# Five low halves written ahead in the output projection, six low halves of the query phase on GpSimd, a fifth head searched early, in a one-core transformer block

## The chip, the cores and the metric

One core of a Trainium2 chip runs the whole block in one launch. The metric is the device time of the program in microseconds, the median over several executions; lower is better. Engines: PE (TensorE, matmuls), DVE (VectorE), ACT (ScalarE), POOL (GpSimd), SP (SyncE, which only issues transfers here).

## The reference

512 tokens of width 1024, in float32. After a mixer, 128 x 128 experts of one neuron each are retrieved for every token by product keys: 8 heads, the 16 best of 128 in each of two halves, the 16 best of their 256 sums.

```python
def reference(x, c, ...):
    ada = silu(c) @ w_ada + b_ada          # shift, scale, gate of both sub-layers
    h = modulate(rmsnorm(x, norm1_g), sh1, sc1)
    z = h @ w_in                            # 2560 columns
    y_a = gate_b * causal_dwconv(gate_c * xa, conv_a_w)
    xr = causal_dwconv(xr, conv_b_w) + conv_b_b
    y_b = rg_lru(xr, ...) * gelu(gr)
    y = concat(head_rmsnorm(y_a), head_rmsnorm(y_b)) @ w_out
    x = x + g1 * y
    h = modulate(rmsnorm(x, norm2_g), sh2, sc2)
    x = x + g2 * peer(h, w_q, sub_keys, expert_u, expert_v)
    return rmsnorm(x, final_g)

def block(xb):                              # of peer, 128 tokens
    q = (xb @ w_q).reshape(p, 8, 2, 64)
    sc = einsum('phcd,hcnd->phcn', q, sub_keys)
    top_s, top_i = top_k(sc, 16)
    ...                                     # the 16 best of 256 sums: idx, g = softmax
    act = gelu(einsum('phkd,pd->phk', expert_u[idx], xb))
    return einsum('phk,phkd->pd', g * act, expert_v[idx])
```

## The kernel before, in words

**Split products.** A float32 product is made from halves: `high` (ACT, line 74) rounds a weight block of 128 x 1024 to fp32r as `whi`, `low` (DVE, line 79) takes `wraw - whi` as `wlo`, and `mm3` multiplies high by high (L88), high by the activations' low (L89) and low by high (L90), for each of 8 pieces of the inner width: 24 matmuls a chunk. `split_w` is high and low in a row. Rings of four buffers hold `wraw`, `whi` and `wlo`.

**Stages in order.**

1. adaLN, norm, the input projection in 20 chunks (`zblock`), the mixer and its head norms, which write `ybuf_h` and `ybuf_l` (L504) in four parts. The parts of adaLN that are needed later (`ada_rest`: rows of `norm2`, and `ada_gate2` for the second gate) go as a generator between other work: pieces of `w_ada` are loaded, multiplied and summed on DVE (L163), summed over partitions by PE (L138), copied by ACT, transposed by PE (L146) and added to `adac` by DVE (L150).
2. The output projection: eight chunks m of `w_out`, 24 matmuls of 512 columns each into `ps_z`. DVE then adds the gated product to the residual, `xs[m]` (L618, for the last chunk L628), ACT squares it, DVE sums the squares (`sqa`, L221). `qsp[0]`, the halves of the first query head, are made behind the loop. Until chunk 6 the program's scheduler places the instructions; the last chunk and the norm behind it stand under a manual schedule, where an engine's order is the order written.
3. The second norm: sums of the squares over partitions (L204), `rs_m` and the reciprocal root (L635 to L640), eight times four transposes of `xs` (L588) for `x1d`, a copy of the residual in DRAM, and the modulated `h2h`, `h2l`, `h2f` (full precision).
4. The query phase: eight heads, each with a chunk of `w_q`, `qT` (ACT, L728), its scores against the keys (L732) and, on DVE, searches of the 16 best (`top16`, L690 to L699: twice MAX8, FIND_INDEX8 and MATCH_REPLACE8 for each half). `qsp[h + 1]` is split during head h. The searches of the first HQ = 4 heads, four tiles of 128 tokens each, are done here (`early`), the others in the next stage.
5. The U phase: 128 chunks of `expert_u` (chunk 0 in the query phase) for the 320 tokens that are computed densely, into `ps_act`, then gelu on ACT. Chunks 1 to FN - 1 = 11 are not split: full float32 matmuls from `h2f` (L1159), which need no work of DVE or ACT on the weights; the others are split. Beside them DVE does the remaining searches, the gates, and dots (L1066) with rows of `expert_u` that POOL gathers (L1045) for the tokens that are computed sparsely. A planner sets the order of this DVE work ahead of time: it adds estimated costs (`pe[0]` by FPE or 3530 ns for a chunk, `dve[0]` by 1140 for a low) and, after each chunk, `turn` picks work as long as DVE's estimated time is behind PE's.
6. The V phase: 128 chunks of `expert_v` into `acc` (L1336 to L1345), for 384 tokens. DVE makes `wlo`, and for two chunks at a time the coefficients `cf` (L1222) and their low half `cl` (L1236); between them stand the remaining dots (L1066) and the weighted sums of gathered rows (L1083), spread evenly. Then the end.

The loads that matter go by SP's queue; gathers and `x1d` by POOL's.

## Time and profile before

| what | us |
|---|---|
| median of 3 runs (1328.17 to 1332.12) | 1329.12 |
| the profiled execution | 1328.57 |
| its span, first to last instruction | 1326.8 |
| mean granted clock of PE, share of full speed | 0.996 |

A row of the page's or a view's timeline reads: start, length, engine, line, operation, output<-inputs, shape, and in brackets the idle time before it and what ended it. Matmuls overlap, so the distance between starts counts and not the length: 0.23 us for 512 columns at the end of the output projection, 0.147 us for the split U chunks. "x8" at a row's end joins eight equal instructions. In the table of stretches every engine has its busy time and, in brackets, its instructions. The page's slices show the stages: PE at 9 from the second slice to the last but one, DMA at 8 or 9 from the eleventh on.

```profile
PE   8999999999999999999999999999999999999995
...
DVE  6889976999999999999999689899899989899998
...
DMA  9765542163898999999999999999999999999993
```

### The profile page before, as it was taken

To read this page: it belongs to the slowest core of one execution; us is meant where nothing else is said; L and a number is where in the kernel's file an instruction comes from. 1 tells how busy PE (TensorE), PEld (TensorE's weight loads), DVE (VectorE), ACT (ScalarE), POOL (GpSimd) and SP (SyncE) were. 2 spreads that over 40 slices of the span, in tenths; PEclk is the share of its full clock that TensorE was granted. 3 is DMA by queue.
4 is the path that set the end of the run, shared out by engine and by line. 5 is a ranking of instruction groups with operands and counts; after the bars stand their busy time and mean duration, and the time that the engine had idled before them with its cause. 6 is when DMAs were issued, how large, how long until landed. Compare 5 with 4: busy or idle time off the path is not lost.

```text
span 1326.8 us, 21286 instructions
## 1 busy us (share of the span) xinstructions
PE 1304.6 (98%) x7506; PEld 1127.3 (85%) x7506; DVE 1215.5 (92%) x2247; ACT 728.2 (55%) x1319; POOL 503.8 (38%) x336
## 2 busy tenths in 40 slices
PE   8999999999999999999999999999999999999995
PEld 6677777777999999999999998788888888888884
DVE  6889976999999999999999689899899989899998
ACT  4677636424586898878669543334343434343432
POOL 0000001000244121446655356677554656554560
PEclk9999999999999999999999999999999999999998
DMA  9765542163898999999999999999999999999993
GB/s 369 272 242 174 185 133 101 59 210 102 302 355 297 341 326 348 394 366 416 417 413 399 402 358 410 377 408 418 412 415 413 415 412 416 412 415 411 416 401 134
DMA packets 150267, 440.05 MB, mean 332 GB/s; under 512 B 16016, under 2 KB 43664, under 8 KB 150160
## 3 DMA queue, kind: packets, MB, share of 16 engines
q1 hardware_dynamic: 103008, 267.23, 53.9%
q0 software_dynamic: 46864, 170.41, 32.5%
q8 instruction: 59, 0.97, 0.3%
q10 hardware_dynamic: 288, 1.05, 0.2%
q14 instruction: 48, 0.39, 0.1%
HBM read 393.54 MB, written 45.09 MB: 331 GB/s over the span
## 4 chain that ended last, share of the span: by engine, by line
PE 56%; DMA 13%; issue 13%; DVE 12%; POOL 3%; ACT 2%; SPq 1%; DVEq 0%; POOLq 0%; ACTq 0%
DMA wraw<-in_v_dram 10%; PE ps_act L88 10%; PE ps_act L89 9%; PE ps_act L90 9%; PE ps_z L89 4%; PE ps_z L90 4%; PE ps_z L88 4%; PE ps_act L1159 4%; PE ps_gt L908 3%; POOL rows L1045 3%; DVE ys L1083 2%; DVE scr L1066 2%; DVE cl L1236 2%; PE acc L1345 2%; DVE wlo L79 2%
## 5 line engine op out<-in xcount | busy, mean ns | idle before, releaser
L74 ACT ACTIVATE whi<-wraw 128x1024 fp32r<-128x1024 f32 x255 | 269.7, 1058 | 217.6 <-DMA wraw<-in_v_dram 148.3
L79 DVE TENSOR_TENSOR wlo<-wraw,whi 128x1024 fp32r<-128x1024 f32 x255 | 310.5, 1218 | 41.9 <-ACT whi L74 41.4
L88 PE MATMUL ps_act<-h,whi 128*128 128x320 f32 x928 | 291.5, 314 | 0.0
L89 PE MATMUL ps_act<-h,whi 128*128 128x320 f32 x928 | 286.8, 309 | 0.0
L90 PE MATMUL ps_act<-h,wlo 128*128 128x320 f32 x928 | 286.7, 309 | 0.0
L1045 POOL DMA_INDIRECT rows<-in_u_dram,idx_s x128 | 204.8, 1600 | 131.1 <-DVE scr L1066 105.4
L1045 POOL DMA_INDIRECT rows<-in_v_dram,idx_s x128 | 197.0, 1539 | 143.8 <-DVE ys L1083 122.4
L1345 PE MATMUL acc<-whi,cl 128*128 128x512 f32 x744 | 230.0, 390 | 1.6 <-DVE cl L1236 1.4
L1345 PE MATMUL acc<-whi,ch 128*128 128x512 f32 x744 | 229.2, 389 | 0.0
L1345 PE MATMUL acc<-wlo,ch 128*128 128x512 f32 x744 | 229.1, 389 | 0.0
L1045 POOL DMA_INDIRECT rows<-in_u_dram,idx_b x64 | 95.7, 1495 | 237.9 <-DVE scr L1066 179.3
L89 PEld LDWEIGHTS ps_act<-h,whi 128*128 128x128 f32 x928 | 174.4, 188 | 0.2
L88 PEld LDWEIGHTS ps_act<-h,whi 128*128 128x128 f32 x928 | 174.2, 188 | 0.3
L90 PEld LDWEIGHTS ps_act<-h,wlo 128*128 128x128 f32 x928 | 174.2, 188 | 0.0
L1345 PEld LDWEIGHTS acc<-whi,cl 128*128 128x128 f32 x744 | 139.1, 188 | 33.0 <-DVE cl L1236 4.5
L1083 DVE SCALAR_TENSOR_TENSOR ys<-rows,acts,ys 128x1024 f32<-128x1024 f32 x127 | 163.3, 1286 | 1.6
L1345 PEld LDWEIGHTS acc<-wlo,ch 128*128 128x128 f32 x744 | 139.7, 188 | 29.1
L1345 PEld LDWEIGHTS acc<-whi,ch 128*128 128x128 f32 x744 | 139.5, 188 | 28.8
L1066 DVE SCALAR_TENSOR_TENSOR scr<-rows,h2n 128x1024 f16<-128x1024 f32 x128 | 156.2, 1220 | 5.3 <-DMA rows<-in_u_dram,idx_s 3.6
L1150 ACT ACTIVATE act<-ps_act 128x320 f32<-128x320 f32 x127 | 55.9, 440 | 125.6 <-PE ps_act L90 92.8
L896 ACT ACTIVATE igh<-oh,gl 128x128 f16<-128x128 f16 x320 | 99.7, 440 | 0.0
L595 POOL DMA_DIRECT2D x1d<-xn x8 | 4.6, 581 | 214.7 <-ACT xn L594 214.7
(325 smaller groups left out, 1921.6 us busy)
## 6 DMA issues: line engine op xcount, KB each, us to landing
wraw<-in_uT_dram SPq DMA_DIRECT2D x120, 512.0 KB, 7.2
wraw<-in_v_dram SPq DMA_DIRECT2D x103, 512.0 KB, 13.4
Gd<-stg SPq DMA_DIRECT2D x46, 512.0 KB, 8.4
wada<-in_w_ada_dram SPq DMA_DIRECT2D x45, 512.0 KB, 6.1
Ad<-act SPq DMA_DIRECT2D x48, 320.0 KB, 6.6
act<-Ad SPq DMA_DIRECT2D x48, 320.0 KB, 15.0
raw<-in_v_dram SPq DMA_DIRECT2D x25, 512.0 KB, 13.4
h<-Gd SPq DMA_DIRECT2D x12, 1024.0 KB, 18.3
```

What stands on the lines that cost most here:

```text
L74: nc.scalar.activation(hi, raw, AF.Copy)
L79: nc.vector.tensor_sub(lo, raw, hi.bitcast(F32))
L88: nc.tensor.matmul(ps, hi[:, k, :], xh(k), start=first and k == ks[0], stop=False)
L89: nc.tensor.matmul(ps, hi[:, k, :], xl(k), start=False, stop=False)
L90: nc.tensor.matmul(ps, lo[:, k, :], xh(k), start=False, stop=last and k == ks[-1])
L896: nc.scalar.activation(ig[:, 1, k // 2, :, k % 2], of[:, k // 2, 0, :, k % 2], AF.Copy, scale=gl[:, t0 + k:t0 + k + 1])
L1045: nc.gpsimd.indirect_dma_start(out=r[:, :], out_offset=None, in_=table, in_offset=bass.IndirectOffsetOnAxis(ap=idxs[:, k:k + 1], axis=0))
L1066: nc.vector.scalar_tensor_tensor(scr, rows.pop(n), 1.0, hn, op0=OP.mult, op1=OP.mult, accum_out=dst[:, k:k + 1])
L1083: nc.vector.scalar_tensor_tensor(ys, rows.pop(k), acts[:, k:k + 1], ys, op0=OP.mult, op1=OP.add)
L1150: nc.scalar.activation(act[c // 2][:, c % 2], ps, AF.Gelu)
L1159: nc.tensor.matmul(ps, raw[:, j, :], h2f[j // 2][:, j % 2], start=j == 0, stop=j == KB - 1)
L1345: nc.tensor.matmul(accs[b][e], st[:, bs], mv[:, e * 512:(e + 1) * 512], start=first, stop=last)
```

## The change

It has five parts.

- `low` and `split_w` can name an engine. In the query phase the low halves of heads 3 to 7 and of U chunk 0 (six) go to GpSimd.
- The output projection is written out under the manual schedule from chunk 1 on. Its first two chunks are split before the loop, `ada_rest` is drained before it, `xs` and the sums of a chunk follow one chunk later, and the second gate is a generator with its pieces loaded two ahead, whose steps stand between the chunks (L195 for L163).
- In it, U chunks 1 to PM = 5 are loaded, split, and their low halves stored in DRAM (`Ld`, 512 KB each) by POOL's queue; `low_ahead` does it.
- In the U phase chunks 1 to 5 are split: the raw block is loaded and rounded by ACT as before for others, the low half is loaded from `Ld` by SP. FN goes from 12 to 14, so full-float32 chunks are now 6 to 13, eight for eleven. The planner's costs follow.
- HQ goes from 4 to 5, with seven search steps in a head for six.

```diff
--- before.py
+++ after.py
@@ -74,14 +74,14 @@
         nc.scalar.activation(hi, raw, AF.Copy)
         return hi
 
-    def low(raw, hi):
+    def low(raw, hi, eng=None):
         lo = wring.tile([128, KB, 128], FR, name="wlo", bufs=WB)
-        nc.vector.tensor_sub(lo, raw, hi.bitcast(F32))
+        (eng or nc.vector).tensor_sub(lo, raw, hi.bitcast(F32))
         return lo
 
-    def split_w(raw):
+    def split_w(raw, eng=None):
         hi = high(raw)
-        return hi, low(raw, hi)
+        return hi, low(raw, hi, eng)
 
     def mm3(ps, hi, lo, xh, xl, ks, first, last):
         for k in ks:
@@ -186,10 +186,20 @@
         yield
 
     def ada_gate2():
-        acc = yield from ada_sum(3, 1)
+        acc = first.pop(3)
+        wts = [None] + [piece(k, 3) for k in (1, 2)]
+        yield
+        nc.vector.tensor_scalar(acc, acc, cl[:, 0:1], None, op0=OP.mult)
+        for k in range(1, KB):
+            yield
+            nc.vector.scalar_tensor_tensor(acc, wts[k], cl[:, k:k + 1], acc, op0=OP.mult, op1=OP.add)
+            if k + 2 < KB:
+                wts.append(piece(k + 2, 3))
         pr = ada_rows()
+        yield
         for b in range(2):
             row_mm(pr, b, ones, acc, True, True)
+        yield
         ada_cols(pr, 40, 8)
         nc.sync.dma_start(g2d.rearrange("b (m p) -> p (b m)", p=128), adac[:, 40:48])
         yield
@@ -458,7 +468,6 @@
                 next(gate1, None)
             next(norm2, None)
             yield
-        yield from ada_gate2()
     ada_it = ada_rest()
 
 
@@ -594,30 +603,53 @@
         nc.scalar.activation(xn, pt, AF.Copy)
         nc.gpsimd.dma_start(x1d[t * 128:(t + 1) * 128, e * 512:(e + 1) * 512], xn)
 
-    osp = {}
-    qraw, qsp = {}, {}
+    osp = {m: split_w(oraw[m]) for m in range(2)}
+    qraw, qsp, uraw = {}, {}, {}
+    Ld = dram.tile([PM, 128, D], F32, name="Ld")
+    for _ in ada_it:
+        pass
+    first[3] = piece(0, 3, "wacc", 2)
+    gate2 = ada_gate2()
+    next(gate2)
+
+    def low_ahead(c):
+        raw = uraw.pop(c)
+        lo = low(raw, high(raw))
+        nc.gpsimd.dma_start(Ld[c - 1], lo.bitcast(F32).rearrange("p k e -> p (k e)"))
+
+    psm = {}
+    norm2 = ExitStack()
     for m in range(KB):
+        if m == 1:
+            norm2.enter_context(tc.manual_schedule())
         if m + 2 < KB:
             oraw[m + 2] = load_w(w_out[m + 2])
         else:
             qraw[m + 2 - KB] = load_w(w_q[m + 2 - KB])
-        if m < KB - 1:
-            osp[m] = split_w(oraw[m])
-        if m >= KB - 2:
-            for _ in ada_it:
-                pass
-            osp[KB - 1] = osp.get(KB - 1) or split_w(oraw[KB - 1])
+        if 1 <= m <= PM:
+            uraw[m] = load_w(uT[m])
         if m == KB - 1:
-            norm2 = ExitStack()
-            norm2.enter_context(tc.manual_schedule())
+            next(gate2)
         hi, lo = osp.pop(m)
-        ps = psZ.tile([128, T], F32, name="ps_z", bufs=3)
-        mm3(ps, hi, lo, lambda k: ybuf_h[:, k, :], lambda k: ybuf_l[:, k, :], kord, True, True)
+        psm[m] = psZ.tile([128, T], F32, name="ps_z", bufs=3)
+        mm3(psm[m], hi, lo, lambda k: ybuf_h[:, k, :], lambda k: ybuf_l[:, k, :], kord, True, True)
+        if m == 0:
+            continue
+        p = m - 1
+        nc.vector.scalar_tensor_tensor(xs[:, p, :], psm.pop(p), adac[:, 16 + p:17 + p], xs[:, p, :], op0=OP.mult,
+                                       op1=OP.add)
+        if 2 <= m + 1 < KB:
+            osp[m + 1] = split_w(oraw[m + 1])
         if m == KB - 1:
-            break
-        nc.vector.scalar_tensor_tensor(xs[:, m, :], ps, adac[:, 16 + m:17 + m], xs[:, m, :], op0=OP.mult, op1=OP.add)
-        sq_sum(m, True)
-        next(ada_it, None)
+            next(gate2)
+        sq_sum(p, True)
+        for _ in range({1: 2, 6: 2}.get(m, 1 if m < 6 else 0)):
+            next(gate2)
+        if m - 1 in uraw:
+            low_ahead(m - 1)
+    if KB - 1 in uraw:
+        low_ahead(KB - 1)
+    ps = psm.pop(KB - 1)
     mx.close()
     adx.close()
     qp = pro.enter_context(tc.tile_pool(name="qp", bufs=2))
@@ -717,7 +749,7 @@
         else:
             qraw[h + 2] = load_w(uT[h - 6])
         if h:
-            qsp[h + 1] = split_w(qraw[h + 1])
+            qsp[h + 1] = split_w(qraw[h + 1], nc.gpsimd if h > 1 else None)
         hi, lo = qsp[h]
         ps = psZ.tile([128, T], F32, name="ps_z", bufs=3)
         mm3(ps, hi, lo, lambda k: h2h[:, k, :], lambda k: h2l[:, k, :], range(KB), True, True)
@@ -731,7 +763,7 @@
             for c in range(2):
                 nc.tensor.matmul(pss[c][:, t, :], qT[64 * c:64 * c + 64, t * 128:(t + 1) * 128],
                                  keys_sb[64 * c:64 * c + 64, h, :], start=True, stop=True)
-        for _ in range(6 if h >= 2 else 0):
+        for _ in range(7 if h >= 2 else 0):
             next(early, None)
         for c in range(2):
             sc[h, c] = scs.tile([128, NT, 128], F32, name="sc", bufs=SCB)
@@ -1100,7 +1132,7 @@
     def w_load(k):
         if k < len(jobs):
             kind, i = jobs[k]
-            if 5 <= k < FN:
+            if 4 + PM < k < FN:
                 raw = wring.tile([128, KB, 128], FR, name=("wlo", "whi")[k % 2], bufs=WB).bitcast(F32)
                 nc.sync.dma_start(raw, uT[i])
                 wraw[k] = raw
@@ -1114,11 +1146,18 @@
                              v[vorder[i] * 128:(vorder[i] + 1) * 128, :].rearrange("p (k e) -> p k e", k=KB))
 
     def w_high(k):
-        if FN <= k < len(jobs):
+        if k <= PM or FN <= k < len(jobs):
             whi[k] = high(wraw[k])
 
+    def low_load(k):
+        if k <= PM:
+            wlo[k] = wring.tile([128, KB, 128], FR, name="wlo", bufs=WB)
+            nc.sync.dma_start(wlo[k].bitcast(F32).rearrange("p k e -> p (k e)"), Ld[k - 1])
+
     def w_low(k):
-        if FN <= k < len(jobs):
+        if k <= PM:
+            wraw.pop(k)
+        elif FN <= k < len(jobs):
             wlo[k] = low(wraw.pop(k), whi[k])
             settle()
 
@@ -1131,6 +1170,7 @@
 
     def weights(k):
         w_ahead(k)
+        low_load(k + 3)
         w_low(k + 2)
 
     act = {0: act0}
@@ -1153,7 +1193,7 @@
         c = jobs[k][1]
         if c:
             ps = pool.tile([128, NU], F32, name="ps_act", bufs=3 if pool is psE else 2)
-            if k < FN:
+            if PM < k < FN:
                 raw = wraw.pop(k)
                 for j in range(KB):
                     nc.tensor.matmul(ps, raw[:, j, :], h2f[j // 2][:, j % 2], start=j == 0, stop=j == KB - 1)
@@ -1164,9 +1204,9 @@
         q = c // 2 - 2
         if c % 2 == 0 and 0 <= q < v0 // 2:
             spill(q)
-        pe[0] += FPE if c and k < FN else 3530
-        dve[0] += 0 if c and k < FN - 2 else 1140
-        ac[0] += 450 if c and k < FN - 3 else 1400
+        pe[0] += FPE if PM < k < FN else 3530
+        dve[0] += 0 if k < FN - 2 else 1140
+        ac[0] += 450 if PM - 3 < k < FN - 3 else 1400
 
     gbuf, g16, gdone = {}, {}, set()
     coef = {}
@@ -1268,6 +1308,7 @@
         w_load(k)
     for k in range(1, 3):
         w_high(k)
+        low_load(k)
     w_low(1)
     manual = ExitStack()
     manual.enter_context(tc.manual_schedule())
@@ -1443,7 +1484,8 @@
 GS = 32768.0
 AB = 3
 GPE = 460
-FN = 12
+FN = 14
+PM = 5
 DX = 0.3
 FPE = 4400
 SE = 0.65
@@ -1468,7 +1510,7 @@
 WB = 4
 WR = 4
 SCB = 8
-HQ = 4
+HQ = 5
 VT = 4
 NW = 32
 
```

What this does to the order of instructions is shown at three places. On DVE as a whole, 278 low halves stand for 281, 51 dots stand ahead of the first `cl` for 47, and 205 of the sparse steps (dots and sums) stand behind it for 209; POOL gets five stores and six subtractions, SP five loads.

**First place, DVE at the start of the output projection.** Before, from the last step of the head norms (L504); the names are those of the stages above.

```order
L163 SCALAR_TENSOR_TENSOR wacc<-wada,cl_104,wacc 128x1024
L504 TENSOR_TENSOR ybuf_l<-mfull,ybuf_h 128x512
L134 MEMSET ps_row 128x512
L618 SCALAR_TENSOR_TENSOR xs<-ps_z,adac,xs 128x512 x3
L79 TENSOR_TENSOR wlo<-wraw,whi 128x1024
L221 TENSOR_TENSOR sqa<-sqa,sq 128x512
L79 TENSOR_TENSOR wlo<-wraw,whi 128x1024
```

And in the changed kernel, where L513 is that step, L639 the `xs` step, L231 the sum of squares and L192 and L195 the second gate:

```order
L513 TENSOR_TENSOR ybuf_l<-mfull,ybuf_h 128x512
L639 SCALAR_TENSOR_TENSOR xs<-ps_z,adac,xs 128x512
L79 TENSOR_TENSOR wlo<-wraw,whi 128x1024
L192 TENSOR_SCALAR wacc<-wacc,cl_104 128x1024
L195 SCALAR_TENSOR_TENSOR wacc<-wada,cl_104,wacc 128x1024
L639 SCALAR_TENSOR_TENSOR xs<-ps_z,adac,xs 128x512
L79 TENSOR_TENSOR wlo<-wraw,whi 128x1024
```

Three `xs` steps stood together behind three chunks that PE worked on in turn; now the first stands alone, and the low half of chunk 2 behind it. The steps of adaLN that stood between those of the head norms (L163) have moved.

**Second place, the end of the output projection.** DVE before, to the second norm's `rs_m`:

```order
L618 SCALAR_TENSOR_TENSOR xs<-ps_z,adac,xs 128x512
L221 TENSOR_TENSOR sqa<-sqa,sq 128x512
L628 SCALAR_TENSOR_TENSOR xs<-ps_z,adac,xs 128x512
L630 TENSOR_TENSOR sq<-xs 128x512
L635 TENSOR_SCALAR rs_m<-ps_col 128x4
```

DVE in the changed kernel, where L660 is the last chunk's `xs` step, L662 its square and L667 `rs_m`; the second low half shown is that of the first query head:

```order
L195 SCALAR_TENSOR_TENSOR wacc<-wada,cl_104,wacc 128x1024 x2
L134 MEMSET ps_row 128x512
L79 TENSOR_TENSOR wlo<-wraw,whi 128x1024
L639 SCALAR_TENSOR_TENSOR xs<-ps_z,adac,xs 128x512
L150 TENSOR_TENSOR adac<-ps_row,small_sb 128x8
L231 TENSOR_TENSOR sqa<-sqa,sq 128x512
L79 TENSOR_TENSOR wlo<-wraw,whi 128x1024
L660 SCALAR_TENSOR_TENSOR xs<-ps_z,adac,xs 128x512
L662 TENSOR_TENSOR sq<-xs 128x512
L667 TENSOR_SCALAR rs_m<-ps_col 128x4
```

PE at the same place before, from the last product:

```order
L90 MATMUL ps_z<-ybuf_h,wlo 128x512
L204 MATMUL ps_col<-ones,sqa 128x1 x4
L588 MATMUL ps_z<-ident,xs 128x128 x8
L204 MATMUL ps_col<-ones,sq 128x1 x4
L588 MATMUL ps_g<-ident,xs 128x128 x8
```

And PE in the changed kernel (L214 for L204, L597 for L588):

```order
L90 MATMUL ps_z<-ybuf_h,wlo 128x512
L146 MATMUL ps_row<-ident,wada 128x128 x4
L214 MATMUL ps_col<-ones,sqa 128x1 x4
L597 MATMUL ps_z<-ident,xs 128x128 x8
L214 MATMUL ps_col<-ones,sq 128x1 x4
L597 MATMUL ps_g<-ident,xs 128x128 x8
```

The second gate's four transposes have moved from the middle of a chunk to behind the last one, and DVE's add that takes them, a sum of squares and a low half stand ahead of the last `xs` step.

**Third place, DVE late in the V phase.** Before, between the 57th and the 58th `cl`:

```order
L1236 TENSOR_TENSOR cl<-cf,ch 128x768
L79 TENSOR_TENSOR wlo<-wraw,whi 128x1024
L1222 TENSOR_TENSOR cf<-act,h_9622 128x2x320
L1083 SCALAR_TENSOR_TENSOR ys<-rows,acts,ys 128x1024 x2
L79 TENSOR_TENSOR wlo<-wraw,whi 128x1024
L1083 SCALAR_TENSOR_TENSOR ys<-rows,acts,ys 128x1024 x2
L1236 TENSOR_TENSOR cl<-cf,ch 128x768
```

And in the changed kernel between the same two (L1276 for L1236, L1262 for L1222, L1115 for L1083):

```order
L1276 TENSOR_TENSOR cl<-cf,ch 128x768
L79 TENSOR_TENSOR wlo<-wraw,whi 128x1024
L1262 TENSOR_TENSOR cf<-act,h_9734 128x2x320
L1115 SCALAR_TENSOR_TENSOR ys<-rows,acts,ys 128x1024
L79 TENSOR_TENSOR wlo<-wraw,whi 128x1024
L1115 SCALAR_TENSOR_TENSOR ys<-rows,acts,ys 128x1024 x2
L1276 TENSOR_TENSOR cl<-cf,ch 128x768
```

One of four sums is gone from this pair of chunks; the rows behind it are as before, up to the end.

## The prediction

> **What bounds the kernel now.** I read the page's busy times first, then the table by stretches, then the list of waits and the rows of single stretches.
>
> ```profile
> PE 1304.6 (98%) x7506; PEld 1127.3 (85%) x7506; DVE 1215.5 (92%) x2247; ACT 728.2 (55%) x1319; POOL 503.8 (38%) x336
> ...
> 200.00:225.00 25.00, 24.09 (x145) 18.25 (x143) 15.62 (x29) 15.15 (x26) 4.63 (x8) 1.00 0.28 106
> 225.00:250.00 25.00, 24.58 (x147) 18.96 (x149) 21.54 (x106) 14.25 (x22) 0.00 (x0) 1.00 0.27 85
> 250.00:275.00 25.00, 25.00 (x149) 20.11 (x148) 25.00 (x152) 7.09 (x13) 0.00 (x0) 1.00 0.24 85
> 275.00:326.00 51.00, 51.00 (x213) 37.07 (x212) 49.20 (x302) 17.07 (x23) 1.12 (x2) 1.00 0.47 153
> 326.00:600.00 274.00, 274.00 (x2156) 270.51 (x2155) 268.97 (x606) 217.75 (x479) 86.76 (x59) 1.00 0.93 338
> 600.00:900.00 300.00, 298.98 (x1918) 276.24 (x1917) 269.84 (x368) 173.83 (x373) 179.53 (x113) 1.00 1.02 400
> 900.00:1200.00 300.00, 299.40 (x1318) 246.64 (x1317) 281.64 (x289) 117.65 (x149) 177.28 (x114) 1.00 1.03 414
> 1200.00:1300.00 100.00, 97.13 (x428) 80.18 (x427) 95.67 (x89) 39.54 (x50) 53.90 (x36) 1.00 1.01 401
> ```
>
> PE is the bound: the columns after the stretch's length are PE, PE's weight loads, DVE, ACT, POOL, granted clock, DMA share, GB/s. From 326 to 1300 PE is idle only 1.0 + 0.6 + 2.9 = 4.5 us, and all of it comes after 600. DVE is the near second: full at 250–275, and 97% in the first split chunks (268.97 of 274). So the change can gain in two ways only: by less PE work, or by removing those 4.5 us. It can lose wherever DVE is made late enough for PE to wait.
>
> **Term 1, three fewer full-precision chunks.** PE work of the U phase:
>
> ```profile
> 279.44 0.81 PE L1159 MATMUL ps_act<-act,wraw 128*128 128x320 f32 x2
> ...
> 326.67 0.55 PE L88 MATMUL ps_act<-h,whi 128*128 128x320 f32 x1
> 327.06 0.31 PE L89 MATMUL ps_act<-h,whi 128*128 128x320 f32 x1
> ...
> 330.57 0.31 PE L89 MATMUL ps_act<-h,whi 128*128 128x320 f32 x1
> ```
>
> The eleven unsplit chunks (1 to 11) take 326.67 − 279.44 = 47.23 us, 4.29 each. A split chunk is 24 matmuls: from the second of one to the second of the next is 330.57 − 327.06 = 3.51. Afterwards eight chunks are unsplit (6 to 13) and three more are split: 3 × (4.29 − 3.51) = **−2.3 us**. Matmuls run back to back here, so the bounds are narrow (−2.2 to −2.4) as long as the low halves are there.
>
> Chunks 1 to 5 get theirs from DRAM: five stores on POOL's queue and five loads on SP's, 512 KB each.
>
> ```profile
> x1d<-xn POOLq DMA_DIRECT2D x8, 256.0 KB, 2.4
> wraw<-in_uT_dram SPq DMA_DIRECT2D x12, 512.0 KB, 3.8
> ```
>
> These are the landing times between 150 and 330 us. Twice the first row is 4.8 us for a store, the second gives 3.8 for a load. Stores come before 207, loads after 270, and the DMA share there is 0.28 to 0.47, so I cost them at nothing. If a load were late, PE would wait for it at one chunk, some 4 us at most.
>
> **Term 2, the output projection and its tail.** What DVE and PE do at its end now:
>
> ```profile
> 197.51 0.17 DVE L150 TENSOR_TENSOR adac<-ps_row,small_sb 128x8 f32<-128x8 f32 x1 [1.75 <-PE ps_row L146]
> ...
> 202.08 0.75 DVE L618 SCALAR_TENSOR_TENSOR xs<-ps_z,adac,xs 128x512 f32<-128x512 f32 x1 [3.81 <-PE ps_z L90]
> 203.59 0.69 DVE L221 TENSOR_TENSOR sqa<-sqa,sq 128x512 f32<-128x512 f32 x1 [0.76 <-ACT sq L219]
> 207.52 0.75 DVE L628 SCALAR_TENSOR_TENSOR xs<-ps_z,adac,xs 128x512 f32<-128x512 f32 x1 [3.24 <-PE ps_z L90]
> 208.30 0.69 DVE L630 TENSOR_TENSOR sq<-xs 128x512 f32<-128x512 f32 x1
> 210.14 0.16 DVE L635 TENSOR_SCALAR rs_m<-ps_col 128x4 f32<-128x4 f32 x1 [1.15 <-PE ps_col L204]
> ```
>
> ```profile
> 196.87 0.60 PE L146 MATMUL ps_row<-ident,wada 128*128 128x128 f32 x4
> ...
> 207.09 0.39 PE L90 MATMUL ps_z<-ybuf_h,wlo 128*128 128x512 f32 x1
> 207.32 0.95 PE L204 MATMUL ps_col<-ones,sqa 128*128 128x1 f32 x8
> ```
>
> ```profile
> L79 DVE TENSOR_TENSOR wlo<-wraw,whi 128x1024 fp32r<-128x1024 f32 x255 | 310.5, 1218 | 41.9 <-ACT whi L74 41.4
> ```
>
> DVE waits 3 to 4 us for PE in each chunk here, so it has room for the five extra lows (5 × 1.22 = 6.1 us). What they cost depends on where they stand. The last xs step (L628) starts 0.2 us after the last product now, and PE's norm work hangs on it, through rs_m at 210.14. In the changed order (the second place shown with the change) four transposes stand behind the last product on PE and DVE has, ahead of that xs step, the gate's add, which waits for those transposes, a sqa add and the low half of the first query head. Counted from 207.32: transposes 0.60, add 0.1, sqa 0.6 (its 0.69 less the overlap seen between neighbours), low 1.14. The xs step starts at 209.8 instead of 207.52: **+2.2**. Nothing covers it, since PE has only those few transposes and sums to do until the norm is ready. The transposes leave the middle of a chunk: −0.45.
>
> Earlier there are two smaller costs. At chunk 2 (first place) the low half of that chunk now stands behind the xs step of chunk 0, whose last products are late in PE's order: 0.75 + 1.2 after it, against about 1.1 until chunk 2 needs it, gives +0.75. That chunk's low was ready early before. At chunk 6 DVE has two gate steps and a memset ahead of PE's row sums, +0.4. Sum 2.2 − 0.45 + 0.75 + 0.4 = **+2.9**. If DVE has caught up at the two early places and only the tail counts, +2.2 less nothing; if each early place costs one whole low more (1.2), some +4.5. I take 2.9, the sum by rows.
>
> **Term 3, the query phase.** Six lows leave DVE, and a fifth head's four tiles are searched there early.
>
> ```profile
> 236.02 0.48 DVE L690 MAX8 top<-sc 128x8 f32<-128x128 f32 x2
> ...
> 238.37 0.28 DVE L690 MAX8 top<-sc 128x8 f32<-128x128 f32 x1
> ...
> 241.88 0.58 ACT L728 ACTIVATE qT<-ps_z 128x512 f32<-128x512 f32 x1
> ...
> 248.64 0.58 ACT L728 ACTIVATE qT<-ps_z 128x512 f32<-128x512 f32 x1
> ```
>
> One tile is 238.37 − 236.02 = 2.35 us, so DVE gets 4 × 2.35 = 9.4 and loses 6 × 1.14 = 6.8: it leaves this phase 2.6 us later against PE. A head lasts 248.64 − 241.88 = 6.76 us, and there is one low in it on GpSimd, which does nothing else then (0.00 in two of the stretches above). No row shows a subtraction on GpSimd. The nearest is DVE's low, 1.22; up to 6.76 it would still fit into one head. From any value between these I get nothing on PE, and I take a price nearer 1.22. The Trainium skill (GPSIMD Engine Reference, § 4.1 Engine selection) speaks against this edit: an elementwise operation with two inputs is to stay on VectorE, since GpSimd takes about twice as long; by that, 2.4 us as an estimate, which is still under a head's time, so its sum is the same, and no run yet shows it.
>
> Does DVE then arrive in time for the first split chunks?
>
> ```profile
> 414.14 1.22 DVE L79 TENSOR_TENSOR wlo<-wraw,whi 128x1024 fp32r<-128x1024 f32 x1
> ...
> 418.96 0.31 PE L90 MATMUL ps_act<-h,wlo 128*128 128x320 f32 x1
> ```
>
> These are the low half of chunk 36 and its first use: it is ready 418.96 − 415.36 = 3.6 us ahead, the smallest margin I found. DVE is 2.6 later, and two lows (chunks 12 and 13) and four tiles of the main part go, but the dots and gates are ordered a chunk or two earlier in exchange. I estimate 0 to 3 us of margin left: **0**.
>
> **Term 4, the V phase.** Four more sparse dots stand ahead of the first V chunk (51 for 47), so 205 sparse steps for 209 are left beside V.
>
> ```profile
> PE acc L1338 <- DVE cl L1236: 2.9, 1, 2.9
> ...
> PE acc L1345 <- DVE cl L1236: 0.4, 1, 0.4
> ```
>
> ```profile
> 1268.20 0.95 DVE L1236 TENSOR_TENSOR cl<-cf,ch 128x768 fp32r<-128x768 f32 x1
> ...
> 1270.94 1.28 DVE L1083 SCALAR_TENSOR_TENSOR ys<-rows,acts,ys 128x1024 f32<-128x1024 f32 x1
> ...
> 1275.79 0.95 DVE L1236 TENSOR_TENSOR cl<-cf,ch 128x768 fp32r<-128x768 f32 x1
> ...
> 1299.56 0.79 PE L1338 MATMUL acc<-whi,cl 128*128 128x512 f32 x1 [2.87 <-DVE cl L1236]
> 1300.15 0.63 PE L1336 MATMUL acc<-whi,ch 128*128 128x512 f32 x1
> 1300.58 0.63 PE L1337 MATMUL acc<-wlo,ch 128*128 128x512 f32 x1
> ```
>
> PE waits for cl, made by DVE once in two chunks. Late in the phase DVE runs without a gap, 7.59 us from one cl to the next with three sparse steps. The last cl is 2.87 us late, and seven further matmuls then come 0.43 us apart rather than 0.23, some 1.6 us more. In the last stretch one pair of chunks carries four steps before and three afterwards (third place): DVE is 1.28 earlier at the end, and the stall shrinks from 2.87 to 1.6. The other three steps stand in the middle, where PE's idle time is 1.0 + 0.6. I take −1.3 there and −1.7 at the end (the stall and a bit of the slow matmuls behind it): **−3.0**. Bounds: 0, if the lateness comes anew from
>
> ```profile
> ACT whi L74 <- DMA wraw<-in_v_dram: 104.1, 46, 6.7
> ```
>
> transfers, which hold ACT's high halves and so DVE's lows between 970 and 1300; and 4.5 + 1.6 = −6.1 if every wait goes.
>
> **Sum.** −2.3 + 2.9 + 0 − 3.0 = −2.4 on the profiled execution's 1328.57 us gives 1326.2. The median of the runs, 1329.12, stands 0.55 above that execution, so **1326.7**.
>
> **Rivals.** *All waits in V go.* For it: they are short, and DVE needs only a few us in all. Against: the DMA share of 1.03 there leaves no faster supply. −2.3 + 2.9 − 6.1 gives 1328.57 − 5.5 + 0.55 = 1323.6, and 1322.9 with the small tail.
>
> *The V phase gains nothing*: the freed steps are refilled by the plan, or DMA sets DVE's lateness; the change then doesn't do on DVE what it says. For it: 104 us of ACT waiting for those transfers. 1328.57 − 2.3 + 2.9 + 0.55 = 1329.7, up to 1331.3 with a tail of 4.5.
>
> *Slower: GpSimd's subtractions hold DVE up.* If DVE stands still for as long as each of the six runs, between one and two lengths of its own low (1.22), it loses 7.3 to 14.6 us while it has no idle time (25.00 of 25). It decides as soon as the loss is over the 3 us of margin: PE then waits 4.3 to 11.6 us at the first split chunks, and the time is 1331.0 to 1338.3. For it: two engines share the same memory, and DVE is full. Against: a DVE search reads a single tile. The Trainium skill (SBUF — State Buffer, § Who interferes with whom) has this as a rule: a DVE instruction with two SBUF inputs contends with a GpSimd instruction that reads SBUF, one with a single input does not; by that, searches (L690) run on and only lows and the like would be held. No row of the profile before shows it.
>
> **How the numbers follow.** A difference of 0.3% (4 us: under 1325.1 or over 1333.1) is about what a measurement of this kernel can tell from none. My forecast 0.50, its own range 1324.5 to 1329.5, of it 0.07 under 1325.1. All V waits gone 0.22, faster. No gain in V 0.13, the same. GpSimd holding DVE 0.15, of it 0.02 the same. Faster 0.29, same 0.58, slower 0.13. The range goes from 1321.5 (all waits gone and a cheaper tail) to 1334 (the lower half of the slower rival).
>
> **What would show it.** Right: eight chunks of 4.29 us at the unsplit line; rs_m some 2.2 us later after the last product; an unchanged head time of 6.76; no PE wait on wlo between 330 and 600; a last cl that is late by about 1.6 us. Wrong: MAX8 or FIND_INDEX8 rows longer than now while a GpSimd row runs beside them; PE waiting for a reloaded wlo at chunks 1 to 5; a last wait as long as before, or gone.

## The result, and the profile after

The changed kernel is slower: 1344.37 us, median of 6 runs (1342.33 to 1346.22), against 1329.90 for the kernel before (6 runs). The ratio is 1.0108, 95% interval 1.0097 to 1.0118. The forecast was 1326.7 with a range to 1334.0, so both the number and the range missed. The profiled execution of the changed kernel has a span of 1340.9 us, 14.1 more than before's 1326.8.

Where the 14.1 us come from is read by setting the same events of both traces side by side. The starts are those of PE's rows.

| event | before | after | later by | step | forecast of the step |
|---|---|---|---|---|---|
| last product of the output projection | 207.09 | 212.95 | 5.9 | +5.9 | +0.7 |
| first product of the query phase | 214.42 | 229.84 | 15.4 | +9.6 | +2.2 |
| first matmul of U chunk 1 | 279.44 | 296.82 | 17.4 | +2.0 | 0 |
| first matmul of U chunk 16 | 341.31 | 356.35 | 15.0 | -2.3 | -2.3 |
| first matmul of V | 770.85 | 787.89 | 17.0 | +2.0 | 0 |
| last matmul of V | 1315.46 | 1329.29 | 13.8 | -3.2 | -3.0 |

Two steps came out with the size that was forecast, the unsplit chunks and the V phase. The loss stands between 160 us, where the first product of the output projection starts in both kernels (159.94 and 159.97), and 250. Two stretches of the changed kernel (columns as in the prediction's table of stretches):

```profile
200.00:225.00 25.00, 16.93 (x93) 12.74 (x93) 10.83 (x19) 4.43 (x8) 2.68 (x5) 0.86 0.48 107
225.00:250.00 25.00, 19.93 (x86) 12.79 (x86) 14.95 (x24) 17.90 (x29) 4.54 (x5) 0.80 0.39 140
```

PE's waits in its whole run (us in sum, how many, the longest):

```profile
PE ps_z L88 <- ACT h L374: 7.5, 2, 7.2
PE ps_row L138 <- DVE ps_row L134: 4.2, 1, 4.2
PE acc L1386 <- DVE cl L1276: 3.0, 3, 2.5
...
PE acc L1379 <- DVE cl L1276: 0.7, 1, 0.7
```

PE was busy 48.7 us of these 50 before and is 36.9 now, and its granted clock falls to 0.86 and 0.80 of full speed. Two new waits carry most of it: 7.2 us at the first query product, for ACT's `h`, and 4.2 us at the row sums of the second gate, for DVE. The wait that closed the V phase before (2.9 us) is down to 0.7. Early in V there is a longer wait for `cl` than before, as the waits between 768 and 900 us show, first in the kernel before and then in the changed one:

```profile
PE acc L1345 <- DVE cl L1236: 1.0, 1, 1.0
```

```profile
PE acc L1386 <- DVE cl L1276: 2.8, 2, 2.5
```

What ACT waited for in the kernel before, and then in the changed one (start, us, what ended its wait in brackets):

```profile
212.28 0.60 ACT L594 ACTIVATE xn<-ps_z 128x512 f32<-128x512 f32 x1 [0.56 <-DMA x1d<-xn]
```

```profile
228.49 0.60 ACT L603 ACTIVATE xn<-ps_z 128x512 f32<-128x512 f32 x1 [8.66 <-DMA x1d<-xn]
228.98 0.80 ACT L374 ACTIVATE h<-mt,adac,A 128x512 fp32r<-128x512 f32 x1
```

What SP had issued shortly before:

```profile
214.01 0.38 SPq L204 DMA_DIRECT2D g2d<-adac  x1
215.74 28.92 SPq L69 DMA_DIRECT2D wraw<-in_w_q_dram  x3
```

The same store on SP in the kernel before:

```profile
197.70 0.38 SPq L194 DMA_DIRECT2D g2d<-adac  x1
```

ACT's fifth `xn` copy needs a buffer that an `x1d` store still reads; there are four. It waits 8.66 us (0.56 before), and the `h` that PE needs stands behind it on ACT. The small store `g2d<-adac`, 4 KB, goes out at 214.01, ahead of the `x1d` stores and the next loads of `w_q`. Before, it went out at 197.70. All that moved in the changed kernel between 216 and 226 us:

```profile
DMA packets 65, 0.27 MB, mean 27 GB/s; under 512 B 0, under 2 KB 0, under 8 KB 65
...
q1 hardware_dynamic: 65, 0.27, 47.4%
```

This is half of the one `w_q` load of 512 KB that SP issued at 215.74. Of the first `x1d` stores, issued from 217.11 on by POOL, nothing moved in these 10 us (their queue, q0, does not appear).

What DVE waited for in the output projection of the changed kernel and in the norm behind it:

```profile
187.98 1.23 DVE L79 TENSOR_TENSOR wlo<-wraw,whi 128x1024 fp32r<-128x1024 f32 x1 [3.35 <-DMA Ld<-wlo]
...
199.05 1.23 DVE L79 TENSOR_TENSOR wlo<-wraw,whi 128x1024 fp32r<-128x1024 f32 x1 [1.52 <-DMA Ld<-wlo]
...
203.50 0.48 DVE L134 MEMSET ps_row<- 128x512 f32 x1
...
215.63 0.74 DVE L660 SCALAR_TENSOR_TENSOR xs<-ps_z,adac,xs 128x512 f32<-128x512 f32 x1
...
218.25 0.16 DVE L667 TENSOR_SCALAR rs_m<-ps_col 128x4 f32<-128x4 f32 x1 [1.15 <-PE ps_col L214]
```

Two low halves wait, 4.9 us together, until a store to `Ld` has landed. So the memset at 203.50 is late, and PE's row sums with it. In that stage, between 185 and 195 us, the DMA share is 0.92, where the kernel before has 0.50.

### The profile page after: what moved, and what is told of

Same layout as the page of the kernel before. It is cut to its first block, busy times and chain, and to the rows that moved or that the text cites. A ratio compares the mean times of both kernels' runs of the same rounds, so it can differ in the third digit from the quotient of the medians.

```text
span 1340.9 us, 21382 instructions
## 1 busy us (share of the span) xinstructions
PE 1305.7 (97%) x7530; PEld 1129.9 (84%) x7530; DVE 1212.6 (90%) x2244; ACT 735.4 (55%) x1327; POOL 511.3 (38%) x347
## 4 chain that ended last, share of the span: by engine, by line
PE 48%; DVE 20%; DMA 17%; issue 10%; ACT 3%; SPq 2%; POOL 1%; DVEq 0%; ACTq 0%; POOLq 0%
DMA wraw<-in_v_dram 9%; PE ps_act L88 8%; PE ps_act L90 8%; PE ps_act L89 8%; PE acc L1386 7%; PE ps_gt L940 3%; DVE ys L1115 3%; DMA rows<-in_u_dram,idx_s 3%; PE ps_z L88 3%; PE ps_z L90 3%; PE ps_z L89 3%; DMA raw<-in_v_dram 2%; DVE wlo L79 2%; DVE cl L1276 2%; DVE scr L1098 2%
## 5 line engine op out<-in xcount | busy, mean ns | idle before, releaser
L74 ACT ACTIVATE whi<-wraw 128x1024 fp32r<-128x1024 f32 x263 | 278.5, 1061 | 234.0 <-DMA wraw<-in_v_dram 126.4
L79 DVE TENSOR_TENSOR wlo<-wraw,whi 128x1024 fp32r<-128x1024 f32 x252 | 306.7, 1218 | 43.6 <-ACT whi L74 38.4
L88 PE MATMUL ps_act<-h,whi 128*128 128x320 f32 x952 | 298.8, 314 | 0.0
L89 PE MATMUL ps_act<-h,whi 128*128 128x320 f32 x952 | 294.2, 309 | 0.0
L90 PE MATMUL ps_act<-h,wlo 128*128 128x320 f32 x952 | 294.2, 309 | 0.0
L1077 POOL DMA_INDIRECT rows<-in_v_dram,idx_s x128 | 194.0, 1516 | 153.6 <-DVE ys L1115 131.6
L88 PEld LDWEIGHTS ps_act<-h,whi 128*128 128x128 f32 x952 | 178.7, 188 | 0.5
L89 PEld LDWEIGHTS ps_act<-h,whi 128*128 128x128 f32 x952 | 178.9, 188 | 0.2
L90 PEld LDWEIGHTS ps_act<-h,wlo 128*128 128x128 f32 x952 | 178.7, 188 | 0.0
L1077 POOL DMA_INDIRECT rows<-in_u_dram,idx_b x64 | 91.9, 1436 | 213.1 <-DVE scr L1098 156.8
L1115 DVE SCALAR_TENSOR_TENSOR ys<-rows,acts,ys 128x1024 f32<-128x1024 f32 x127 | 163.4, 1287 | 1.4
L1269 ACT ACTIVATE ch<-cf 128x768 fp32r<-128x768 f32 x64 | 54.2, 847 | 67.0 <-DVE cf L1262 28.9
```

The costliest lines, as they stand in the source:

```text
L74: nc.scalar.activation(hi, raw, AF.Copy)
L79: (eng or nc.vector).tensor_sub(lo, raw, hi.bitcast(F32))
L88: nc.tensor.matmul(ps, hi[:, k, :], xh(k), start=first and k == ks[0], stop=False)
L89: nc.tensor.matmul(ps, hi[:, k, :], xl(k), start=False, stop=False)
L90: nc.tensor.matmul(ps, lo[:, k, :], xh(k), start=False, stop=last and k == ks[-1])
L1077: nc.gpsimd.indirect_dma_start(out=r[:, :], out_offset=None, in_=table, in_offset=bass.IndirectOffsetOnAxis(ap=idxs[:, k:k + 1], axis=0))
```

## The experiments

### The moved store

Theory A: the gate's store keeps the transfer engines busy, and what stands behind it is late. Rival B: the five low-half stores on POOL's queue delay the `x1d` stores. Rival C: SP's queue is held while it waits for `adac`.

**First run: the kernel before, the store moved to the tail.**

```diff
-        nc.sync.dma_start(g2d.rearrange("b (m p) -> p (b m)", p=128), adac[:, 40:48])   # in ada_gate2
...
     stat(sq, False, True)
+    g2c = const.tile([128, 8], F32, name="g2c")
+    nc.vector.tensor_copy(g2c, adac[:, 40:48])
+    nc.sync.dma_start(g2d.rearrange("b (m p) -> p (b m)", p=128), g2c)
```

> The kernel before, with one thing moved: the store of the second gate (g2d, 4 KB in pieces of 4 bytes) is issued behind the last xs step of the output projection instead of at 197.5 us. Theory A (the scattered store keeps the transfer engines busy for some 9 to 11 us, and what is issued behind it, the x1d stores first, lands late): ACT waits 6 to 9 us for x1d<-xn, PE waits 5 to 8 us at the first products of the query phase, median 1335 to 1340. Rival B (the five low-half stores on POOL's queue delay the x1d stores) and rival C (SP's queue is held while it waits for adac): no change, 1328 to 1331.

Measured: 1355.97 us, ratio 1.0184 (1.0163 to 1.0205). PE waited 7.8 us at the first query products, and U began 10.6 us later than before. ACT's wait:

```profile
ACT xn L593 <- DMA x1d<-xn: 9.2, 1, 9.2
```

These are the waits that theory A forecast, with nothing else of the change in the kernel. The total was beyond every expectation: the V phase took 15.6 us more as well.

**Second run of the store: the same without the new tile.**

```diff
-    g2c = const.tile([128, 8], F32, name="g2c")
-    nc.vector.tensor_copy(g2c, adac[:, 40:48])
-    nc.sync.dma_start(g2d.rearrange("b (m p) -> p (b m)", p=128), g2c)
+    nc.vector.tensor_copy(adac[:, 40:48], adac[:, 40:48])
+    nc.sync.dma_start(g2d.rearrange("b (m p) -> p (b m)", p=128), adac[:, 40:48])
```

> The kernel before with the g2d store behind the output projection, as in the first run, but without that run's new tile of 32 bytes a partition: DVE copies the eight columns onto themselves ahead of the store. In the first run the query phase began 9.3 us late, and 15.6 us more were lost in the V phase, where the program is the same. If the V phase's loss came from the new tile (every later tile lies 32 bytes further), it is gone here: 1339 to 1343, ACT's wait for x1d<-xn 9 us as there. If it came from the moved store, it is here again: 1354 to 1358.

Measured: 1341.51 us, ratio 1.0083 (1.0056 to 1.0110); U began 10.9 us late, V was 1.8 us longer than before. So the store alone costs some 11 us here, and V's 15.6 us came with the tile. Packets of all queues over the store's 9 us in the kernel before (197.4 to 206.6), and over 11.5 us around its issue at 208.77 in this run (208.5 to 220):

```profile
DMA packets 1041, 0.02 MB, mean 2 GB/s; under 512 B 1040, under 2 KB 1040, under 8 KB 1040
...
q1 hardware_dynamic: 1040, 0.00, 5.3%
```

```profile
DMA packets 1145, 0.37 MB, mean 32 GB/s; under 512 B 1056, under 2 KB 1056, under 8 KB 1145
...
q0 software_dynamic: 105, 0.36, 88.7%
q1 hardware_dynamic: 1040, 0.00, 4.1%
```

The store's 4 KB go out as 1040 packets, about one for each of its 1024 elements. Before, nothing else was under way in that time but one packet of instructions. Here 0.36 MB of `x1d` (queue q0) take 88.7% of the time of 16 engines for 11.5 us, in which at the rate of the V phase (414 GB/s) 4.8 MB would move. So theory A has to be put more exactly: the store's own packets take only 4.1% of the engines' time (in the kernel before all 1040 lie between 198.6 and 199.6 us, though the store lands at 206.64), and it is the packets behind it that are slow. The Trainium skill (DMA: Bandwidth & Descriptors, § Rules for kernel authors) says that a pattern whose last dimension isn't contiguous becomes one descriptor for each element; the packet count agrees. The same page of the Trainium skill (§ Back-pressure in remote DMA) says, of transfers between cores, that stalled writes stall an engine's other queues too; q0 behind q1's store looks like it, but that it is the same mechanism is not shown.

**The changed kernel, the store at U chunk 7.**

```diff
         w_high(k + 3)
+        if k == 7:
+            nc.sync.dma_start(g2d.rearrange("b (m p) -> p (b m)", p=128), adac[:, 40:48])
```

> The changed kernel with the g2d store issued at U chunk 7 instead of behind the output projection. Theory A: ACT's wait for x1d<-xn falls from 8.7 us to under 1, PE's wait at the first query products from 7.2 to under 1; median 1344.4 less 7 to 10, 1334 to 1337. Rival B: both waits stay, 1343 to 1346. Rival C gives the same as A here; the next run parts them.

Measured: 1334.16 us, ratio to before 1.0019 (1.0005 to 1.0032). PE's wait at the first query products is 0.7 us, and ACT's is nearly gone:

```profile
ACT xn L602 <- DMA x1d<-xn: 0.3, 1, 0.3
```

The low-half stores are still in this kernel, so B is out.

**The same, and at the old place a store of the same 4 KB in rows of 32 bytes.**

```diff
-        nc.sync.dma_start(g2d.rearrange("b (m p) -> p (b m)", p=128), adac[:, 40:48])
+        nc.sync.dma_start(g2x, adac[:, 40:48])      # g2x: [128, 8] in DRAM
```

> As the run before, but at the old place, with the same wait for adac, SP stores the same 4 KB in another layout, 32 bytes a partition in one piece, into a tensor that nothing reads; the real store stays at U chunk 7. Theory A (the number of 4-byte pieces): as the run before, 1334 to 1337. Rival C (SP's queue held for adac): as the changed kernel, 1343 to 1346, with the waits at x1d<-xn and at the first query products back.

Measured: 1336.18 us, 1.0039 (1.0026 to 1.0053), ACT's wait 0.3 us. The intervals of this run and the last touch, and both are 8 us or more under the changed kernel. SP waits for `adac` here as in the change (it issues this store 1.06 us behind the last product in both), so C is out: what costs is that the 4 KB go out in single elements.

### The low halves written ahead

**The changed kernel without them.**

```diff
-PM = 5
+PM = 0
-FN = 14
+FN = 12
```

> The changed kernel without the low halves written ahead (PM 0, FN 12: no loads, halves and stores of U chunks 1 to 5 in the output projection, eleven unsplit chunks as before), g2d store as in the change. Theory A: the output projection ends 4 to 5 us earlier (DVE no longer waits for Ld stores), the 7 us wait behind it stays, the unsplit chunks cost 2.3 more: 1341 to 1344. Rival B: the wait behind it goes as well: 1332 to 1335.

Measured: 1339.38 us, 1.0055 (1.0036 to 1.0073). ACT still waits 6.5 us for `x1d<-xn`, PE 3.5, so the wait behind the projection is not theirs. The output projection ends at 208.43 for 212.95, but in this execution it also began later, its first product at 162.10 for 159.97. Counted from the first product it takes 46.3 us for 53.0, so the low halves cost 6.7 us where they are made (5.4 and 7.8 in the two runs above, which have them too; before it took 47.2).

**Without them and with the store at U chunk 7.** Both edits together.

> The changed kernel without the low halves written ahead and with the g2d store at U chunk 7. Theory (two separate costs, the low halves' transfers in the output projection and the store's behind it): both go; what is left is the order of the new output projection, +1.3 at its last product and +2.2 behind it, less some 2 to 3 in the V phase: 1331 to 1333 where before has 1331.75. Rival (the rewritten order itself is the loss, whatever is transferred): 1336 or more, with U's first product still 6 us or more later than before.

Measured: 1330.27 us, 0.9995 (0.9981 to 1.0008): no difference from before. The last product is at 206.36, 0.7 us earlier than before, so the rewritten order by itself loses nothing there. The two costs are separate, and with both gone the loss in the total is gone. U begins 4.2 us late all the same, and V is 3.1 us shorter. Of the 4.2, some 2.2 are the tail of the prediction's term 2. Another 2.6 are new, and the projection gives back the 0.7: from the last product to the first `qT` this run takes 29.6 us, the run with the halves and the late store 27.0. The stretches of both runs from about 4 to 12 us behind the last product, this run first:

```profile
210.00:218.00 8.00, 7.46 (x38) 7.43 (x38) 2.47 (x8) 3.46 (x8) 2.94 (x5) 0.57 0.60 229
```

```profile
219.00:227.00 8.00, 6.71 (x50) 5.54 (x50) 5.02 (x13) 5.63 (x12) 3.23 (x6) 1.00 0.61 242
```

PE's granted clock is 0.57 here and 1.00 there. Both runs have the same two short waits of PE just ahead (0.9 and 0.5 us), so what lowers the clock in one of them is not shown.

**Halves made, nothing stored.** Loads and splits of U chunks 1 to 5 stay; the store is left out, and the halves are not used (eleven unsplit chunks).

> The changed kernel with the g2d store at U chunk 7 and eleven unsplit chunks, where the output projection loads and splits U chunks 1 to 5 as in the change but stores nothing (the halves are not used). It parts what made that stage's last product 5.9 us late. Theory (the stores: their transfers, and wlo buffers that stay taken until a store has landed): the last product within 1.5 us of before's 207.1, as without the halves (206.4): 1329 to 1332. Rival (ten more instructions on ACT and DVE and five more loads): 212 or later, 1334 or more.

Measured: 1330.85 us, 1.0000 (0.9989 to 1.0012); last product at 206.20. Five more loads, rounds and subtractions cost nothing. The stores do.

**Stores alone.** This run does not test what it was meant to: with nothing ahead of them on POOL's queue that made them wait, its stores from `ybuf_h` went out at 111 us, long before the stage, so it says nothing about the stage.

> The same kernel with the opposite half: no loads and no halves of U chunks ahead, but five stores of 512 KB on POOL's queue at the same places, from a tile that is there anyway (ybuf_h), into a tensor that nothing reads. No buffer of wlo waits for them. Theory (a wlo buffer that waits for its store): last product at 207 to 208, 1329 to 1332. Rival (the share of DMA that the stores take, so that w_out and w_ada come late): 210 or later, ACT and DVE waiting for transfers, 1333 or more.

Measured: 1331.49 us, 1.0005 (0.9993 to 1.0017).

**All transfers, no buffer that waits.** Halves as above, and five stores of the same size at the change's places, from finished slices of `xs`, into a tensor that nothing reads.

```diff
         lo = low(raw, high(raw))
+        nc.gpsimd.dma_start(Lx[c - 1], xs[:, c - 1:c + 1, :].rearrange("p k t -> p (k t)"))
```

> The kernel with loads and halves of five U chunks in the output projection and no use of them, now with five stores of 512 KB on POOL's queue at the change's places, but from xs (two finished slices each), which nobody overwrites. All the change's transfers are there, and no wlo buffer waits for them. Theory (a wlo buffer that stays taken until its store has landed): last product at 206 to 208, 1329 to 1332. Rival (the transfers themselves, so that w_out and w_ada come late): 210 to 213, ACT and DVE waiting for loads, 1334 to 1337.

Measured: 1332.15 us, 1.0018 (1.0002 to 1.0034); last product at 207.07, as before (46.9 us from the first). A stretch of that stage in this run:

```profile
185.00:195.00 10.00, 10.00 (x46) 8.29 (x45) 8.94 (x10) 4.52 (x6) 1.06 (x2) 1.00 1.03 417
```

What ACT waited for in it:

```profile
ACT whi L74 <- DMA wraw<-in_w_out_dram: 6.2, 3, 3.2
```

The DMA share is as high as in the V phase of the kernel before (1.03; it was 0.92 in the changed kernel's same stretch), and ACT waits 6.2 us for `w_out` in the stage, but PE is busy for all of these 10 us, and its longest wait in the stage is 0.9 us. So it is not the transfers: it is the `wlo` buffer. A ring of four hands a buffer to a later low half only when the store from it has landed. In the changed kernel the first store goes out at 179.56 and DVE goes on at 187.98, some 8 us later, and in this order the products' low halves stand behind it. The wait stands at the third low half behind the stored one; by a ring of four one would look for it at the fourth, and why it stands one earlier is not shown.

### The query phase by itself

**The kernel before with six low halves on GpSimd and the fifth head's searches.**

> The kernel before with only the query phase's part of the change: six low halves on GpSimd, a fifth head searched early. Theory: 2.4 us each on GpSimd, hidden under a head of 6.76; U begins when it did (279.4, within 0.3 us); DVE has four sparse steps less beside the V phase: 2 to 3 us faster than before. Rival of the prediction (GpSimd's subtractions hold DVE up): MAX8 and FIND_INDEX8 longer than 0.28 beside them, waits of PE for wlo in the first split chunks, 4 us or more slower.

Measured: 1329.03 us against 1330.98, 0.9987 (0.9971 to 1.0004), which is not clear of no difference; the profiled span is 1.9 us shorter. GpSimd's low halves in this run (their least, median and greatest ns):

```profile
L79 POOL TENSOR_TENSOR wlo<-wraw,whi x6: 2370/2377/2388, 228.9 to 255.4; 128x1024 fp32r<-128x1024 f32 x6
```

DVE's searches between 225 and 330 us in it (busy us, mean ns, idle time ahead), and then in the kernel before:

```profile
L690 DVE MAX8 top<-sc 128x8 f32<-128x128 f32 x62 | 14.8, 280 | 6.2 <-ACT sc L738 6.2
```

```profile
L690 DVE MAX8 top<-sc 128x8 f32<-128x128 f32 x56 | 13.4, 281 | 0.0
```

A subtraction takes 2.38 us on GpSimd, 1.95 times DVE's 1.22, and hides under a head. The Trainium skill's "~2× slower" (GPSIMD Engine Reference, § 4.1 Engine selection) agrees. MAX8 takes 280 ns in this stretch, where some of its rows stand beside a subtraction, and 281 without any, so nothing holds the searches up. That is what the Trainium skill's rule on shared reads (SBUF — State Buffer, § Who interferes with whom) gives for one input. The prediction's slower rival is out.

**Only the subtractions on GpSimd, HQ 4.**

> The kernel before with six low halves of the query phase on GpSimd and nothing else (HQ 4). Theory (the gain beside V comes from the four searches moved ahead): nothing in the query phase, DVE idles there, V's time within 1 us of before's, 1330 to 1333. Rival (freeing DVE in the query phase is enough, the planner moves dots ahead by itself): V 2 us shorter as with the fifth head, 1328 to 1330.

Measured: 1330.95 us against 1330.41, 1.0006 (0.9995 to 1.0016). From V's first to its last matmul it took 547.6 us, the run before it 541.9, the kernel before 544.6. With the subtractions alone V's last wait for `cl` is 2.8 us, as before; with the fifth head it is not there. So the gain in V comes with the fifth head, not with the subtractions. These are single executions, but the others agree: fourteen profiled kernels with the fifth head spend 539.6 to 544.6 us in V, the three without it and without a new tile 544.6 to 547.6.

### Versions meant to beat both

**Low halves of U chunks 1 to 5 made ahead in the query phase, on GpSimd (FN 12).**

> The run before this one, and the low halves of U chunks 1 to 5 made ahead in the query phase instead of the output projection, on GpSimd too (two subtractions a head, 4.8 of 6.76 us), and stored from there, where the DMA share is 0.24 to 0.33; FN stays 12, so six unsplit chunks for eleven. Theory: 5 x 0.78 = 3.9 us less on PE, nothing lost in the output projection: 3 to 7 us faster than before. Rival (the transfers cost wherever they stand): the query phase or the first U chunks longer by 3 us or more, no gain.

**The same, the high halves in the low halves' own buffers (FN 12, then 14).**

> The earlier kernel with U's low halves made ahead on GpSimd in the query phase, with one thing mended: there, the high halves of those chunks took buffers of whi, so that ACT stood before a qT until PE let one go (PE waited 9.4 us for qT). Here ACT writes the rounded block into the low half's own buffer and GpSimd subtracts in place. Theory: PE's waits for qT go, U begins at 279 to 281, six unsplit chunks for eleven save 3.9 us: 1323 to 1327. Rival (DVE, relatively later by those 3.9 us, makes PE wait in the first split chunks, or the query phase stays longer): 1329 or more.

> The same with FN 14, eight unsplit chunks for eleven as in the change: 2.3 us saved on PE, and DVE has two low halves less. Theory: 1.6 us slower than FN 12 if DVE is in time there, 1325 to 1329; equal or faster than it if DVE was late.

Measured: 1340.94 us (1.0066; 1.0043 to 1.0088), 1335.64 (1.0042; 1.0024 to 1.0060) and 1335.99 (1.0041; 1.0026 to 1.0057). All three are slower, and all three show the same new wait of PE (4.9 us in sum in the third); in the first two:

```profile
PE ps_g L739 <- ACT qT L735: 9.4, 3, 3.8
```

```profile
PE ps_g L741 <- ACT qT L737: 5.1, 2, 3.7
```

ACT's extra roundings stand ahead of `qT` in its order and wait there (in the first run 25.5 us in sum for GpSimd's low halves; in the second mostly for something that the profile doesn't name), and PE waits for `qT`. U began 16.7, 9.0 and 7.7 us late, so these waits are only part of the loss. In the second run its first five chunks then saved 3.9 us.

**The changed kernel's tail mended, without low halves ahead.** The gate's row sums go between the pieces of the last chunk, its transposes ahead of the last piece, the query head's low half behind the last `xs` step.

> The changed kernel without low halves ahead (eleven unsplit chunks) and with the g2d store at U chunk 7, its tail mended: the row sums of the second gate after four of the last chunk's eight pieces, its transposes after seven, and the first query head's low half behind the last xs step and its square. Without the mending U began 4.2 us later than before. Theory (the prediction's tail, +2.2, and as much again from it): U begins 0 to 2 us later than before, 1326 to 1329. Rival (the loss lies in the rest of the new order): 4 us as before, 1330.

**That, with three low halves ahead, in every other chunk.**

> The mended tail with three U chunks' low halves made ahead in every other chunk of the output projection (PM 3, FN 12: eight unsplit chunks), so that a wlo buffer has twice the time and the stores half the rate. Theory: last product at 207 to 209, 2.3 us less in U: 1324 to 1328, the fastest of these. Rival (stores hold wlo buffers even so): last product at 210 or later, 1329 or more.

Measured: 1330.88 us (0.9994; 0.9983 to 1.0005) and 1333.20 (1.0013; 0.9999 to 1.0027). The last `xs` step stands 0.44 us behind the last product again (2.68 in the changed kernel), but U begins 4.1 us late as without the mending: now a `w_q` load, issued at 209.83, goes out among the first `x1d` stores, ACT waits 3.0 us for `x1d<-xn`, and PE 1.6 us at the first query product. With three halves ahead the projection ends at 206.03, so a `wlo` buffer with twice the time costs nothing. U's first chunks save 2.4 us there, and by V 6.3 us are lost again; PE's largest new wait in U:

```profile
PE ps_gt L945 <- DVE igh L926: 2.5, 3, 1.7
```

Both expectations were too low, and no version beats the kernel before by more than a measurement can tell.

### Where tiles lie

**The kernel before with the first run's tile and the copy into it, nothing moved; then with 64 bytes for 32.**

```diff
+    g2c = const.tile([128, 8], F32, name="g2c")     # then [128, 16]
+    nc.vector.tensor_copy(g2c, adac[:, 40:48])
```

> The kernel before with the first run's tile of 32 bytes a partition and the copy into it (0.1 us), and nothing moved. If the V phase's 15.6 us came from where the later tiles lie: 1343 to 1347, the loss between V's first and last matmul. If that took the moved store as well: 1329 to 1332.

> The run with nothing but a new tile of 32 bytes a partition, with one of 64 bytes instead. If what counts is whether the later tiles begin at a multiple of 64 bytes: as before, 1329 to 1333, V from first to last matmul 544 to 546 us. If any shift does it: 1342 to 1348, 560 us or more.

Measured: 1346.16 us, 1.0105 (1.0085 to 1.0125), and 1345.38, 1.0116 (1.0101 to 1.0131). Up to V both are within 0.5 us of before; V takes 562.9 and 561.1 us for 544.6. No engine's order differs but for that copy. The middle of V with 32 bytes:

```profile
900.00:1200.00 300.00, 291.14 (x1263) 238.13 (x1262) 268.78 (x279) 111.17 (x142) 170.77 (x109) 0.99 1.03 399
```

PE's waits for `cl` in its whole run:

```profile
PE acc L1347 <- DVE cl L1238: 10.9, 9, 2.3
```

The DMA share is the same 1.03, but it moves 399 GB/s for 414. 64 bytes are no better than 32, so it is not the multiple of 64. Nor is it the copy: the second run of the store has a copy and no tile, and its V takes 546.4 us. The tile stands in the kernel's first pool, so it may move all tiles behind it, but no run reads their addresses. What it is stays open.

## Why the prediction was wrong, step by step

**Term 1 (three fewer unsplit chunks, -2.3)** was right: from U chunk 1 to chunk 16 the changed kernel gains 2.3 us. Its step that the five stores and loads cost nothing failed. It read the DMA share and the landing times from the kernel before; in the changed kernel the share in that stage was 0.92, and the first store took some 8 us for a forecast 4.8. The share by itself was not what cost (1.03 without a loss where the stores come from `xs`). The step left out that a stored `wlo` buffer stays taken until its store has landed, in the ring that the products' low halves use. Counted from its first product, the output projection takes 53.0 us in the changed kernel and 46.3 without stored halves: this step costs 6.7 us (5.4 to 7.8 over the three kernels that have it). The projection's end is only 5.9 us late because the new order by itself is 0.9 us shorter than the old one (47.2).

**Term 2 (+2.9)** had two parts. The small early costs (+0.7) were not there: the same order without stores that hold buffers takes 46.3 to 46.9 us from its first product, before it took 47.2. The tail came out to a tenth: the last `xs` step 2.68 us behind the last product for 0.43 (+2.25), `rs_m` 5.30 for 3.05, as worked out (+2.2). But the step counted the gate's transposes, its add and a low half, and not the transfer that the same generator issues, though its 8.9 us to landing can be read from the trace of the kernel before. Moving the add moved the store from a time without other transfers to just ahead of the `x1d` stores. From the last product to the first `qT` the changed kernel takes 36.3 us, with the store elsewhere 27.0, the kernel before 24.8: **the store is 9.3 us, the tail's order 2.2**. Some 2 of the 9.3 come behind PE's wait: from the first query product to the first `qT` it takes 19.41 us for 17.45 before, at a granted clock of 0.80 from 225 to 250 us. This is the step that failed most: a transfer that the prediction put at nothing by not listing it.

**Term 3 (0)** was right for the query phase: 6.76 us a head in both, GpSimd 2.38 us for an estimated 2.4, no search slower. In U the forecast 0 was 2.0 too low. PE waits in no place longer than 0.6 us there; with the fifth head and the subtractions alone 0.9 of the 2.0 are there too, with the subtractions alone none, and the rest is not explained. Of the versions with less PE work at U's start, the two with six unsplit chunks gave back 3.8 and 5.5 us between chunk 16 and V, the last one 5.9, and the one with FN 14 only 1.0; some of it stands in waits for DVE's gate operands. DVE's margin there may have been smaller than the 0 to 3 us that I estimated. That is argued, not shown.

**Term 4 (-3.0)** came out as -3.2, but not from its two parts, and so partly by luck. The forecast had -1.3 in the middle and -1.7 at the end. From V's first matmul to the one ahead of the last wait the changed kernel takes 0.4 us more (525.89 for 525.45), since it has the wait of 2.5 us early in V; from there to the last matmul it takes 3.7 us less (15.51 for 19.16). The row at the last wait:

```profile
1314.88 0.50 PE L1379 MATMUL acc<-whi,cl 128*128 128x512 f32 x1 [0.71 <-DVE cl L1276]
1315.22 0.40 PE L1377 MATMUL acc<-whi,ch 128*128 128x512 f32 x1
1315.45 0.39 PE L1378 MATMUL acc<-wlo,ch 128*128 128x512 f32 x1
```

The wait is 0.7 us for a forecast 1.6, and the slow matmuls behind it (0.43 us apart before) are gone. The runs with and without the fifth head give the end's gain to that head (a last wait of 2.8 us without, none with it); that it is the four dots, and not something else that moves with the head, is argued. One execution of each differs by 5.7 us in V, more than forecast.

**The rivals.** The slower rival had the right sign and the wrong mechanism: nothing on GpSimd held DVE. The true one, a transfer moved onto the path, was in none of them, and the range ended at 1334 since no term allowed for a late transfer.
